# Joint steps of the second MLP product: the weight splits of a pair are ordered behind its first copy, and two slot splits move to a later place

## The chip, the cores and the metric

The kernel runs on one core of a Trainium2 chip. The metric is the device time of one execution in microseconds (us); the kernel before was timed three times, with a median of 2363.1 us (2361.05 to 2365.14).

The engines that matter here are TensorE (PE in the profile: matmuls, with their weight loads as PEld), VectorE (DVE), ScalarE (ACT), GpSimd (POOL, here only an issuer of DMAs) and SyncE (SP, which issues the weight loads).

## The reference

One decoder layer over 528 tokens of width 2048 (16 meta tokens and 512 real ones), in float32. Two token mixers are merged, and an MLP follows. The change touches only the second matrix product of that MLP.

```python
u2 = rmsnorm(h, norm2_g[l])
h = h + jnp.square(jax.nn.relu(u2 @ mlp_w1[l])) @ mlp_w2[l]
out = rmsnorm(h, final_g)
return out[:, N_META:]
```

`mlp_w1` is 2048 x 8192 and `mlp_w2` is 8192 x 2048. Calling the first product MLP 1 and the second MLP 2, MLP 2 is the stretch from about 1717 us to 2335 us of the profile.

## The kernel before, in words

**Three matmuls for one.** A float32 matmul is done with both operands split into a high part in a shorter format and a low remainder. `whi` and `wlo` are the parts of a weight block. A split costs one ScalarE copy (`whi <- raw`, line 154) and one VectorE subtraction (`wlo <- raw, whi`, line 155). The product is then high by high, high by low and low by high (`mm3`, line 396 in the profile).

**Seven products for eight.** The big products are done two by two blocks at a time with Winograd's form of Strassen's method. A group of four weight blocks a, b, c, d yields seven weight operands, in this order: a; s = c + d; s = s + a; b; c = c + a; s = s + b; d. The additions are on VectorE (line 142). Counting from 0, these are called split 0 to split 6. The seven products bear the name of the token-side operand: x11, t1, t2, x21, t3, x22, t4. They accumulate in the PSUM banks A, B, A, C, A, B, A. Results leave as follows: after x11 bank A is copied to `p1` (ScalarE); after t1 bank B is copied to `q5`; after t2 bank A is copied to `u2`; after x21 `put("11")` adds C and `p1`; after t3 `put("22")` combines A and `q5`; after x22 `put("12")` adds B and `u2`; after t4 `put("21")` is a negated copy on ScalarE.

**The weight stream.** The class `Weights` (lines 48 to 188) knows the loads and splits of the whole kernel in order. `next()` hands out the next pair of parts. `advance()` makes sure that the splits are traced up to two beyond the ones used. There are four buffers each for the loaded raw blocks, for `whi` and for `wlo`, and two for the sums. Each split that is traced also traces the loads that have a free buffer, on SyncE.

**MLP 2.** A step t takes a column of products along a diagonal. It uses the slots `max(0, t-8)` to `min(t, 31)-1`: step 1 has one slot, step 8 has eight. A slot holds the squared activations of two column blocks of MLP 1, in all the forms x11, t1 and so on. The slots come back from HBM by DMA (`load_slot`) and are split in place by `split_slot` (lines 1116 to 1121): one copy on ScalarE (line 1120) and one subtraction on VectorE (line 1121) for each of the pieces `x11` (256 columns), `late` (768: t1, x21, x22) and `soon` (768: t2, t4, t3).

**Joint steps.** Steps with few slots are done in pairs by `strassen_pair`, so that one split weight block serves both: first [1, 3] and [2, 4], and at the end [32, 38], [33, 37] and [34, 36]; between them come single steps 5 to 31 by `strassen`, and step 35 at last. In a pair the first step has `p1`, `u2`, `q5` in buffers of its own. The second step has them in the tile `scale`: its `p1` and its `q5` share one half of it, so that the copy of `q5` has to wait until `put("11")` has read `p1`. `scale` also holds the norm factor `rho` that MLP 1 reads until its last column. Below, "pair [1, 3]" and "pair [2, 4]" are the first two, and "step 3" the second step of the first of them.

**What precedes.** The last column of MLP 1 (j = 31, `strassen_turned`) starts MLP 2's work through the hooks in `last` (line 1127): it loads slots 1 to 3, splits slots 1 and 2, and after its last product traces four splits of weights ahead (`W.ready(W.used + 4)`). Its squared result `y` is stored by a DMA from a buffer that the results `e` of step 3 take over.

**The order on an engine.** The source isn't the order of execution. The framework arranges each engine's instructions when the program is built: of those that it deems ready it takes the one that comes first in the source, and one from further down goes ahead when nothing earlier is ready. In the trace, for instance, products of bank C of step 1 stand between two parts of a product in bank A. Each engine then executes its list in that order. `tc.issue_after(x)` adds an order: what the block traces on the engine of x is put behind x in that engine's list. It adds nothing on other engines.

**The places of the change.** `strassen_pair` (from line 795) calls `W.advance()` after each product. After the copy of `u2` it calls `between()`, which is `split_slot(n + 3)` (line 1202): slot 3 in pair [1, 3], slot 4 in pair [2, 4], and nothing in the last three pairs, where n + 3 is past the last slot. Slot 3 is first used by step 4 (second in pair [2, 4]), slot 4 by step 5. Results of the first two pairs are added to HBM in three pieces each by DMAs on POOL (line 1193), and a step's `e` buffer is free for a later step when these have landed.

Of the kernel before, what the change touches and what calls it, by code (L numbers as in the profile page):

```python
# [190 lines left out]
def build(ctx, tc, nc, xt_d, par_d, w_in_d, gate_d, pool_d, woa_d, wob_d, woc_d, w1_d, w2_d, w2t_d,  # L191
# [10 lines left out]
    W = Weights(nc, wpool, sums_pool, 4, 4)  # L202
# [82 lines left out]
    jobs = "V2_0 VL_2 VR_0 VL_3 GA_0 VP_2 GA_1 VP_3 VL_4 PW_0 VL_5 F_0 VP_4 GA_2 VP_5 F_1 VL_6 VP_6 VL_7 F_2"  # L285
    jobs += " VP_7 GA_3 VL_8 PW_1 F_3 VL_9 F_4 VP_8 GA_4 VP_9 VL_10 F_5 VP_10 VL_11 F_6 VP_11 GA_5 VL_12 PW_2 F_7"
    jobs += " VL_13 VP_12 GA_6 VP_13 VP_14 VL_14 VL_15 VP_15 GA_7 PW_3"
    jobs = [(j.split("_")[0], int(j.split("_")[1])) for j in jobs.split()]
# [35 lines left out]
    def slots_of(t):  # L324
        return range(max(0, t - WIN), min(t, JS))
# [67 lines left out]
    def mm3(o, w, mh, ml, first, last):  # L393
        wh, wl = w
        for i, (a, b) in enumerate(((wh, mh), (wh, ml), (wl, mh))):
            done = PE.matmul(o, a, b, start=first and i == 0, stop=last and i == 2, skip_group_check=True)  # L396
        return done
# [282 lines left out]
    def bank(name, j, n=HS):  # L680
        return ps.tile([P, 512], F32, tag="ps", name=f"ps_{name}{j}")[:, :n]
# [110 lines left out]
        put("21", E, u2)  # L792
        W.advance()

    def strassen_pair(names, jobs, puts, between):
        n = range(2)
        base = (0, len(jobs[0]("x11")))
        A, B, C = ([bank(x, name) for name in names] for x in "ABC")
        spare = {"p1": scale[:, :HS], "u2": scale[:, HS:SEQ], "q5": scale[:, :HS]}
        p1, u2, q5 = ([ep.tile([P, HS], F32, tag=x, name=f"{x}_{names[0]}"), spare[x]] for x in ("p1", "u2", "q5"))  # L800

        def product(os, r, first):
            hi, lo = W.next()
            for i in n:
                xs = jobs[i](r)
                for k, x in enumerate(xs):
                    s = slice((base[i] + k) * P, (base[i] + k + 1) * P)
                    mm3(os[i], (hi[:, s], lo[:, s]), *x, first and k == 0, k == len(xs) - 1)

        def put(c, os, zs):  # L810
            for i in n:
                puts[i](c, os[i], zs[i])

        def copy(os, xs):
            return [S.activation(o, x, AF.Copy) for o, x in zip(os, xs)][-1]

        product(A, "x11", True)
        copy(p1, A)
        W.advance()
        product(B, "t1", True)  # L820
        copy(q5[:1], B)
        W.advance()
        product(A, "t2", False)
        with tc.issue_after(copy(u2, A).ins):
            between()
        W.advance()
        product(C, "x21", True)
        put("11", C, p1)
        copy(q5[1:], B[1:])
        W.advance()  # L830
        product(A, "t3", False)
        put("22", A, q5)
        W.advance()
        product(B, "x22", False)
        put("12", B, u2)
        W.advance()
        product(A, "t4", False)
        put("21", A, (None, None))
        W.advance()

    def put_plain(e, by_half=False):

        def put(c, x, z):
            a, b = int(c[0]) - 1, int(c[1]) - 1
            n = 1 - a + 2 * b if by_half else 2 * a + b
            o = e[:, n * HS : (n + 1) * HS]
            if c[0] == "1":
                V.tensor_tensor(o, x, z, op=ALU.add)
            elif z is None:
                S.activation(o, x, AF.Copy, scale=-1.0)  # L850
            else:
                V.scalar_tensor_tensor(o, x, -1.0, z, op0=ALU.mult, op1=ALU.subtract)
        return put
# [238 lines left out]
    slots, early, n = {}, late.enter_context(ExitStack()), 14 * HS  # L1092
# [4 lines left out]
    def load_slot(j, queue):  # L1097
        if j < JS:
            s = slots[j] = places[j % (WIN + 1)]
            if j % (WIN + 1) in odd_places:  # L1100
                queue.dma_start(s[:, : 6 * HS].bitcast(F32), y_sp[j][:, : 6 * HS])
                queue.dma_start(s[:, 6 * HS + ODD : 7 * HS + ODD].bitcast(F32), y_sp[j][:, 6 * HS :])
            else:
                queue.dma_start(s[:, : 7 * HS].bitcast(F32), y_sp[j])

    def slot(j, r):

        s, odd = slots[j], j % (WIN + 1) in odd_places
        if r == "x11":
            lo = 6 * HS + (ODD if odd else 0)  # L1110
            return s[:, lo + HS : lo + 2 * HS], s[:, lo : lo + HS]
        a = {None: slice(0, 6 * HS), "late": slice(3 * HS, 6 * HS), "soon": slice(0, 3 * HS)}.get(r) or at(r)
        h = 8 * HS + (64 if odd else 0) + a.start
        return s[:, h : h + a.stop - a.start], s[:, a]

    def split_slot(j):
        if j < JS:
            for r in ("x11", "late", "soon") if j <= WIN else (None, "x11"):
                hi, lo = slot(j, r)
                S.activation(hi, lo.bitcast(F32), AF.Copy)  # L1120
                V.tensor_tensor(lo, lo.bitcast(F32), hi.bitcast(F32), op=ALU.subtract)
# [58 lines left out]
    def pair(q):  # L1180
        return ht[:, q].rearrange("p b a s -> p (b a s)")

    def of_slots(t):
        return lambda r: [slot(j, r) for j in slots_of(t)]

    def adding(e, p):
        put = put_plain(e, True)

        def put_and_add(c, x, z):
            put(c, x, z)  # L1190
            at = {"22": slice(HS, 3 * HS), "12": slice(3 * HS, 4 * HS), "21": slice(0, HS)}.get(c)
            if at:
                nc.gpsimd.dma_start(h_sp[p][:, at], e[:, at], accum_op=ALU.add)
        return put_and_add

    last = []
    for n, g in enumerate(groups):
        t = g[0]
        if len(g) > 1:
            es = [yp.tile([P, 2 * SEQ], F32, tag="ty"[i], name=f"e{x}") for i, x in enumerate(g)]  # L1200
            puts = [adding(e, x % WIN) if n < 2 else put_plain(e, True) for e, x in zip(es, g)]
            strassen_pair([f"b{x}" for x in g], [of_slots(x) for x in g], puts, lambda: split_slot(n + 3))
        else:
            es = [yp.tile([P, 2 * SEQ], F32, tag="yt"[t % 2], name=f"e{t}")]
            strassen(f"b{t}", of_slots(t), put_plain(es[0], True), between=lambda: split_slot(t) or [f() for f in last[::-1]])
        if n >= 2 and t < JS + 2:
            for x, e in zip(g, es):
                nc.gpsimd.dma_start(h_sp[x % WIN], e, accum_op=ALU.add)
        if n < 4:
            load_slot(n + 5, nc.gpsimd)  # L1210
        elif t >= WIN:
            load_slot(t + 1, nc.gpsimd)
        if t == JS + 2:
            ends.close()
            hp = ctx.enter_context(tc.tile_pool(name="hp2", bufs=1, reuse_waits="tile"))
            ht = hp.tile([P, KD // 2, 2, 2, HS], F32, name="acc")
            for q in (2, 0, 1, 3, 4, 5, 6, 7):
                nc.gpsimd.dma_start(pair(q), h_sp[ORDER[q]])
        if t >= JS + 2:
            for x, e in zip(g, es):  # L1220
                V.tensor_tensor(pair(x - JS), pair(x - JS), e, op=ALU.add)
        if t == JS + 2:
            fs, free = [], slots[25]
            for i, m in enumerate(range(2 * JS, 64)):
                yl, fh, fl = (free[:, (3 * i + x) * SEQ : (3 * i + x + 1) * SEQ] for x in range(3))
                nc.gpsimd.dma_start(yl.bitcast(F32), y_sp[m // 2][:, slice(0, SEQ) if m % 2 else slice(SEQ, 2 * SEQ)])
                fs.append((fh, fl))

                def split_last(yl=yl.bitcast(F32), fh=fh, fl=fl):
                    S.activation(fh, yl, AF.Copy)  # L1230
                    V.tensor_tensor(fl, yl, fh.bitcast(F32), op=ALU.subtract)
                last.append(split_last)
# [6 lines left out]
    n = 64 - 2 * JS  # L1239
# [121 lines left out]
```

## Time and profile before

| | |
|---|---|
| median of three runs | 2363.1 us |
| lowest and highest | 2361.05 and 2365.14 us |
| the profiled execution's own time | 2362.76 us |
| its span, first to last instruction | 2361.0 us |
| mean granted TensorE clock | 0.997 |
| PE busy, share of the span | 99% |
| DVE, ACT, POOL | 82%, 51%, 13% |

A row of the timeline gives start, duration, engine, line of the kernel, operation, output and inputs by the program's names with the numbers left out (`ps_Ab` is bank A of any step b1, b2 and so on), shapes, and how many were merged; in brackets the idle time of the engine before it and what ended that. The view of waits gives the total, the count and the longest. The view of windows gives the busy time of each engine in a stretch, with the number of instructions.

### The profile page before, as it was taken

The numbers are of one execution on the slowest core, as the hardware profiler recorded it, in microseconds if no ns is written. First come the engines' busy times: TensorE is split into PE (matmuls) and PEld (weight loads), VectorE is DVE, ScalarE is ACT, GpSimd is POOL, SyncE is SP. The second block draws the span as 40 slices with busy tenths as digits, with TensorE's granted clock in tenths as the row PEclk, the third lists the DMA queues.
The fourth block names the chain that finished last, engine by engine and source line by source line (L and its number), as shares of the span: only waits on it lengthen the run. The fifth ranks groups of instructions, "written<-read, shape, count | busy, mean of one in ns | idle before, by whom it ended". The sixth has DMA issues, their size and how long they took to land.

```text
span 2361.0 us, 46354 instructions
## 1 busy us (share of the span) xinstructions
PE 2334.7 (99%) x19274; PEld 2290.5 (97%) x19274; DVE 1927.0 (82%) x2375; ACT 1212.2 (51%) x1641; POOL 318.5 (13%) x439
## 2 busy tenths in 40 slices
PE   9999999999999999999999999999989999999997
PEld 9999999999999999888999999999989999999997
DVE  7866766698888886378989888888889888888877
ACT  6654545455555554244545444444455555555554
POOL 0224343300000000032000000000020000000013
PEclk9999999999999999999999999999999999999999
DMA  6255555754444447468545444555486666666663
GB/s 206 85 169 179 173 176 173 260 202 150 147 157 153 150 153 263 166 214 286 171 154 160 158 155 158 165 163 165 162 245 175 181 183 184 193 191 188 175 197 107
DMA packets 117442, 418.73 MB, mean 177 GB/s; under 512 B 14288, under 2 KB 19792, under 8 KB 115568
## 3 DMA queue, kind: packets, MB, share of 16 engines
q1 hardware_dynamic: 77472, 253.40, 33.5%
q0 software_dynamic: 39616, 162.29, 21.2%
q8 instruction: 150, 2.46, 0.4%
q14 instruction: 60, 0.49, 0.1%
q10 hardware_dynamic: 144, 0.10, 0.0%
HBM read 324.89 MB, written 90.31 MB: 176 GB/s over the span
## 4 chain that ended last, share of the span: by engine, by line
PE 86%; DVE 5%; issue 3%; DMA 2%; ACT 2%; POOL 2%; SPq 0%; POOLq 0%; ACTq 0%; DVEq 0%
PE ps_A L396 14%; PE ps_Ab L396 14%; PE ps_B L396 7%; PE ps_Bb L396 7%; PE ps_vp L396 5%; PE ps_vl L396 4%; PE ps_wo L396 4%; PE ps_Agp L396 4%; PE ps_Age L396 4%; PE ps_C L396 4%; PE ps_Agl L396 3%; PE ps_Cb L396 3%; PE ps_Bgp L396 2%; PE ps_Bgl L396 2%; PE ps_Bge L396 2%
## 5 line engine op out<-in xcount | busy, mean ns | idle before, releaser
L154 ACT ACTIVATE whi<-raw 128x1024 fp32r<-128x1024 f32 (+5 forms) x391 | 399.7, 1028 | 312.5 <-issue 80.4
L155 DVE TENSOR_TENSOR wlo<-raw,whi 128x1024 fp32r<-128x1024 f32 (+5 forms) x391 | 467.4, 1198 | 113.3 <-ACT whi L154 109.6
L154 ACT ACTIVATE whi<-sum 128x1024 fp32r<-128x1024 f32 (+3 forms) x267 | 279.0, 1045 | 449.3 <-DVE sum L142 231.0
L155 DVE TENSOR_TENSOR wlo<-sum,whi 128x1024 fp32r<-128x1024 f32 (+3 forms) x267 | 319.9, 1198 | 70.3 <-ACT whi L154 65.4
L396 PE MATMUL ps_A<-a,whi 128*128 128x256 f32 x2000 | 346.3, 277 | 0.6 <-ACT p L714 0.6
L396 PE MATMUL ps_Ab<-a,whi 128*128 128x256 f32 x1728 | 304.9, 277 | 0.0
L396 PEld LDWEIGHTS ps_A<-a,whi 128*128 128x128 f32 x2000 | 301.5, 188 | 1.4 <-ACT p L714 0.8
L396 PE MATMUL ps_A<-a,wlo 128*128 128x256 f32 x1000 | 276.5, 276 | 0.1
L396 PEld LDWEIGHTS ps_Ab<-a,whi 128*128 128x128 f32 x1728 | 260.9, 188 | 0.1
L396 PE MATMUL ps_Ab<-a,wlo 128*128 128x256 f32 x864 | 239.0, 277 | 0.0
L142 DVE TENSOR_TENSOR sum<-sum,raw 128x1024 f32<-128x1024 f32 (+4 forms) x178 | 213.7, 1201 | 5.7
L396 PEld LDWEIGHTS ps_A<-a,wlo 128*128 128x128 f32 x1000 | 187.7, 188 | 0.3 <-DVE wlo L155 0.3
L396 PE MATMUL ps_B<-a,whi 128*128 128x256 f32 x1024 | 177.7, 276 | 0.0
L396 PEld LDWEIGHTS ps_Ab<-a,wlo 128*128 128x128 f32 x864 | 162.5, 188 | 0.0
L396 PE MATMUL ps_vp<-a,whi 128*128 128x272 f32 (+1 forms) x896 | 160.4, 282 | 0.1
L396 PE MATMUL ps_vl<-a,whi 128*128 128x272 f32 (+1 forms) x896 | 160.2, 282 | 0.0
L396 PE MATMUL ps_wo<-a,whi 128*128 128x512 f32 x512 | 158.1, 390 | 0.0
L396 PEld LDWEIGHTS ps_B<-a,whi 128*128 128x128 f32 x1024 | 154.2, 188 | 0.2 <-ACT whi L154 0.2
L396 PE MATMUL ps_Bb<-a,whi 128*128 128x256 f32 x864 | 152.1, 276 | 0.0
L396 PE MATMUL ps_B<-a,wlo 128*128 128x256 f32 x512 | 141.5, 276 | 1.0 <-DVE wlo L155 1.0
L396 PEld LDWEIGHTS ps_vl<-a,whi 128*128 128x128 f32 x896 | 137.7, 188 | 0.2
L396 PEld LDWEIGHTS ps_vp<-a,whi 128*128 128x128 f32 x896 | 137.5, 188 | 0.3 <-ACT gs L540 0.3
(353 smaller groups left out, 5847.5 us busy)
## 6 DMA issues: line engine op xcount, KB each, us to landing
raw<-w SPq DMA_DIRECT2D x168, 512.0 KB, 4.2
raw<-w_in SPq DMA_DIRECT2D x134, 512.0 KB, 3.7
w<-w SPq DMA_DIRECT2D x56, 512.0 KB, 4.2
a<-ysp POOLq DMA_DIRECT2D x20, 896.0 KB, 6.2
ysp<-t POOLq DMA_DIRECT2D x31, 512.0 KB, 4.9
hsp<-e POOLq DMA_DIRECT2D x29, 512.0 KB, 5.8
w<-w_in SPq DMA_DIRECT2D x24, 512.0 KB, 4.0
ysp<-y POOLq DMA_DIRECT2D x31, 384.0 KB, 5.0
```

The source lines that it names most:

```text
L142: nc.vector.tensor_tensor(self.raw[o], self.raw[x], self.raw[y], op=ALU.add)
L154: nc.scalar.activation(hi[:, s], raw[:, s], AF.Copy)
L155: nc.vector.tensor_tensor(lo[:, s], raw[:, s], hi[:, s].bitcast(F32), op=ALU.subtract)
L396: done = PE.matmul(o, a, b, start=first and i == 0, stop=last and i == 2, skip_group_check=True)
```

## The change

`strassen_pair` gets one more argument, `when`. The `advance()` behind the first product is traced inside `issue_after` of the second step's `p1` copy. `between()` is still ordered behind the `u2` copy, but it is called at one of five places: 0 behind that copy as before, 1 behind result 11, 2 behind result 22, 3 behind result 12, 4 behind result 21. Pair [1, 3] takes 3, pair [2, 4] takes 4, and the last three pairs take 0.

```diff
-    def strassen_pair(names, jobs, puts, between):
+    def strassen_pair(names, jobs, puts, between, when):
...
+        def done(n, copied):
+            if n == when:
+                with tc.issue_after(copied.ins):
+                    between()
+
         product(A, "x11", True)
-        copy(p1, A)
-        W.advance()
+        with tc.issue_after(copy(p1, A).ins):
+            W.advance()
         product(B, "t1", True)
         copy(q5[:1], B)
         W.advance()
         product(A, "t2", False)
-        with tc.issue_after(copy(u2, A).ins):
-            between()
+        copied = copy(u2, A)
+        done(0, copied)
         W.advance()
         product(C, "x21", True)
         put("11", C, p1)
         copy(q5[1:], B[1:])
+        done(1, copied)
         W.advance()
         product(A, "t3", False)
         put("22", A, q5)
+        done(2, copied)
         W.advance()
         product(B, "x22", False)
         put("12", B, u2)
+        done(3, copied)
         W.advance()
         product(A, "t4", False)
         put("21", A, (None, None))
+        done(4, copied)
         W.advance()
...
-            strassen_pair(..., lambda: split_slot(n + 3))
+            strassen_pair(..., lambda: split_slot(n + 3), dict(enumerate((3,4))).get(n, 0))
```

More of the change, by code (lines that the diff above doesn't have):

```diff
@@ L1201, in build @@
             puts = [adding(e, x % WIN) if n < 2 else put_plain(e, True) for e, x in zip(es, g)]
-            strassen_pair([f"b{x}" for x in g], [of_slots(x) for x in g], puts, lambda: split_slot(n + 3))
+            strassen_pair([f"b{x}" for x in g], [of_slots(x) for x in g], puts, lambda: split_slot(n + 3), dict(enumerate((3,4))).get(n, 0))
         else:
```

## The prediction

> **What bounds the kernel now.** I read the page first, then the view of waits for TensorE, and then windows and timelines of the first joint steps.
>
> ```profile
> PE 2334.7 (99%) x19274; PEld 2290.5 (97%) x19274; DVE 1927.0 (82%) x2375; ACT 1212.2 (51%) x1641; POOL 318.5 (13%) x439
> ```
>
> ```profile
> PE ps_Bb L396 <- ACT scale L815: 2.4, 1, 2.4
> PE ps_Ab L396 <- ACT p_b L815: 2.3, 1, 2.3
> PE ps_Ab L396 <- DVE e L852: 1.6, 2, 1.2
> PE ps_Ab L396 <- ACT scale L815: 1.2, 1, 1.2
> ```
>
> TensorE is the bound, and nearly all that it loses in MLP 2 is lost in these four rows, 7.5 us together. The windows (columns: stretch, length, busy time with count per engine, granted clock, DMA share, GB/s) show where.
>
> ```profile
> core 0: us, PE busy (x) PEld busy (x) DVE busy (x) ACT busy (x) POOL busy (x), PEclk, DMA share, GB/s
> 1720.90:1743.70 22.80, 19.14 (x145) 18.33 (x145) 18.83 (x30) 16.45 (x32) 6.92 (x9) 0.93 0.95 268
> 1743.70:1750.90 7.20, 4.82 (x42) 4.63 (x42) 7.18 (x13) 1.37 (x4) 2.63 (x3) 1.00 0.51 131
> 1750.90:1762.10 11.20, 10.92 (x94) 10.71 (x93) 9.92 (x16) 8.39 (x15) 2.64 (x3) 1.00 0.99 229
> 1762.10:1794.00 31.90, 30.62 (x268) 30.43 (x268) 29.68 (x37) 18.33 (x28) 1.72 (x2) 1.00 0.59 162
> 1794.00:2344.00 550.00, 550.00 (x4834) 549.67 (x4835) 461.95 (x496) 292.20 (x406) 59.07 (x84) 1.00 0.60 176
> 1725.70:1729.40 3.70, 3.63 (x18) 3.64 (x19) 2.40 (x5) 3.10 (x8) 1.60 (x3) 0.55 0.92 297
> ```
>
> From 1794 on TensorE has no idle time for 550 us. What the change can win lies between 1720.9 and 1794, and there VectorE has little to spare: 7.18 of 7.20 us is busy in the second stretch and 29.68 of 31.90 in the fourth. In the last row 18 matmuls take 3.63 us at a granted clock of 0.55. At the rate of the long stretch (550.00 us over 4834, 0.114 us each) they would take 2.05, so the clock's fall behind the first two stalls costs 1.6 us more.
>
> **Part 1, the splits behind the first product's copy.** Pair [1, 3] has nothing in that block. The last hook of MLP 1 has already traced four splits ahead, and the `advance()` behind x11 asks for fewer. Its stalls look like this:
>
> ```profile
> 1722.28 0.63 ACT L154 ACTIVATE whi<-sum 128x512 fp32r<-128x512 f32 x1 [3.03 <-DVE sum L142]
> 1722.82 0.37 ACT L815 ACTIVATE p_b<-ps_Ab 128x256 f32<-128x256 f32 x1
> ...
> 1723.24 0.50 PE L396 MATMUL ps_Ab<-slot,whi 128*128 128x256 f32 x2 [2.32 <-ACT p_b L815]
> ...
> 1725.77 0.55 PE L396 MATMUL ps_Ab<-slot,whi 128*128 128x256 f32 x2 [1.19 <-ACT scale L815]
> ```
>
> The copy `p_b` stands behind a split that waits 3.03 us for a VectorE sum. That split was traced by the hook and not in the block, so it keeps its place, and 2.32 + 1.19 us of stall and the 1.6 us of slow clock stay. Moreover the product that waits, t2, uses this very split, which ends at 1722.28 + 0.63 = 1722.91. Cost and gain here: 0.
>
> In pair [2, 4] the block holds split 2, and that one already follows the copy:
>
> ```profile
> 1736.27 0.38 ACT L815 ACTIVATE scale<-ps_Ab 128x256 f32<-128x256 f32 x1
> 1736.53 0.85 ACT L154 ACTIVATE whi<-sum 128x768 fp32r<-128x768 f32 x1
> ```
>
> Again 0. In each of the last three pairs it does change the order. Here is pair [32, 38]:
>
> ```profile
> 2252.63 1.06 ACT L154 ACTIVATE whi<-sum 128x1024 fp32r<-128x1024 f32 x1 [2.64 <-DVE sum L142]
> ...
> 2253.73 1.23 DVE L155 TENSOR_TENSOR wlo<-sum,whi 128x1024 fp32r<-128x1024 f32 x1 [0.88 <-ACT whi L154]
> ...
> 2257.19 1.06 ACT L154 ACTIVATE whi<-w 128x1024 fp32r<-128x1024 f32 x1
> 2258.15 0.36 ACT L815 ACTIVATE scale<-ps_Ab 128x256 f32<-128x256 f32 x1
> ...
> 2259.77 0.39 PE L396 MATMUL ps_Ab<-a,whi 128*128 128x256 f32 x2
> 2259.99 0.28 PE L396 MATMUL ps_Ab<-a,wlo 128*128 128x256 f32 x1
> ```
>
> Split 2 is done at 2252.63, some 7 us before t2 needs it at 2259.77. The change puts it behind the copy into `scale`. That copy can start when x11 is done, about 2257.19 (there split 4 takes the buffer that x11 frees). Copy 0.36, `whi` 1.06 and `wlo` 1.23 end at 2259.84. The first third of t2's first block needs only `whi` (2258.61), and `wlo` is asked for at 2259.99: just in time. So the value that I take is 0, but the cover is gone. One VectorE instruction of 1.2 us in front makes it 1.1 late. If split 2 also finds its `whi` buffer taken by a later split, it waits until t1 is done (2259.77), and t2's `wlo` comes at 2259.77 + 1.06 + 1.23 = 2262.06, 2.1 late. TensorE can do x21 meanwhile, which has its own bank and weights; bounds are thus 0 and 2.1 per pair, 0 and 6.3 for three. A gain is excluded, as TensorE has no idle time there. I take 0, since the copy is short and the framework can turn products round.
>
> **Part 2, slot 3 behind result 12 of pair [1, 3].** No DMA moves with it, and POOL's adds and SP's loads keep their place in their own lists. On ScalarE it is still behind the `u2` copy, where nothing else is ready. On VectorE it now comes after results 11, 22 and 12:
>
> ```profile
> 1728.12 1.87 ACT L1120 ACTIVATE a<-a 128x256 fp32r<-128x256 f32 x3
> ...
> 1729.90 2.16 DVE L1121 TENSOR_TENSOR a<-a 128x256 fp32r<-128x256 f32 x3
> 1732.32 0.43 DVE L848 TENSOR_TENSOR e<-ps_Cb,scale 128x256 f32<-128x256 f32 x1 [0.26 <-DMA ysp<-y]
> ```
>
> The three subtractions (2.16 us) stand ahead of step 3's result 11, but that one waits 0.26 us longer for the store of MLP 1's last `y`, whose buffer it takes. So nothing is won on it: 0. Results of step 1 may go up to 2 us sooner, and with them the first adds to HBM; the slot's pieces come later by as much, for step 4's x11, which has other products in front. Bounds, as estimates: 1.0 won (sooner adds, half of those 2 us, since the later adds still follow their products) to 0.5 lost (one 0.42 us piece of the slot awaited); I take 0.
>
> **Slot 4 behind result 21 of pair [2, 4].** This is the step that matters.
>
> ```profile
> 1743.72 0.42 DVE L848 TENSOR_TENSOR e<-ps_Cb,p_b 128x256 f32<-128x256 f32 x1 [1.75 <-PE ps_Ab L396]
> 1744.06 0.42 DVE L1121 TENSOR_TENSOR a<-a 128x256 fp32r<-128x256 f32 x1
> 1744.39 0.95 DVE L155 TENSOR_TENSOR wlo<-raw,whi 128x768 fp32r<-128x768 f32 x1
> 1745.26 1.82 DVE L1121 TENSOR_TENSOR a<-a 128x768 fp32r<-128x768 f32 x2
> 1747.00 0.42 DVE L848 TENSOR_TENSOR e<-ps_Cb,scale 128x256 f32<-128x256 f32 x1
> ...
> 1747.45 0.39 ACT L815 ACTIVATE scale<-ps_Bb 128x256 f32<-128x256 f32 x1 [3.43 <-DVE e L848]
> ...
> 1747.89 0.50 PE L396 MATMUL ps_Bb<-slot,whi 128*128 128x256 f32 x2 [2.38 <-ACT scale L815]
> ```
>
> Step 4's result 11 (1747.00) frees `scale` for the `q5` copy, which frees bank B for x22: 0.89 us from the one to TensorE. Two subtractions of slot 4 (1745.26 to 1747.00) stand in front. Behind result 21 they come later, and result 11 starts at 1745.26: 1.74 us sooner, and the stall of 2.38 shrinks to 0.64. With the small piece gone too it is 0.33.
>
> But VectorE's work is only turned round. It is full until 1750.90, and the slot must be split before step 5 reaches its fifth slot. What is late next is step 5's weights:
>
> ```profile
> 1750.51 0.74 ACT L154 ACTIVATE whi<-sum 128x640 fp32r<-128x640 f32 x1
> 1751.28 0.83 DVE L155 TENSOR_TENSOR wlo<-sum,whi 128x640 fp32r<-128x640 f32 x1 [0.34 <-ACT whi L154]
> 1753.84 0.83 DVE L155 TENSOR_TENSOR wlo<-sum,whi 128x640 fp32r<-128x640 f32 x1 [0.87 <-ACT whi L154]
> ...
> 1762.13 0.50 PE L396 MATMUL ps_Ab<-slot,whi 128*128 128x256 f32 x2 [0.31 <-DVE e L852]
> ...
> 1793.97 0.50 PE L396 MATMUL ps_Ab<-slot,whi 128*128 128x256 f32 x2 [1.25 <-DVE e L852]
> ```
>
> At 1762.13 and 1793.97 TensorE waits for VectorE anyway. VectorE can be earlier there only by idle time that it loses: 11.20 - 9.92 = 1.28 us at most before 1762.1. The 0.34 is a wait for ScalarE, which stands behind a result of TensorE's that now comes sooner, so it goes; the 0.87 is a chain of sum, copy and subtraction and may stay. Kept: 0.34 to 1.28, and I take 0.8, the middle. The rest of the 1.74 comes back as waits for `wlo` in step 5 or for result 22 after it.
>
> Sum: 0 + 0 + 0 - 0.8. The profiled execution's 2362.76 becomes 2362.0; the median of the runs lies 0.3 above it, so 2362.3.
>
> On the clock, the Trainium skill ("TensorE: Matmul & The Clock Gate", Why this matters for your kernels) warns of "PE-idle gaps >~3µs between matmul bursts". By it neither the stalls here nor a late pair's 2.1 us would cost any clock; the trace disagrees, since gaps of 2.32 and 1.19 us sufficed for the 0.55.
>
> **The rivals.**
> *The whole stall is kept.* If step 1's earlier adds let VectorE start sooner than 1743.72 (it idles 1.75 us there), or the framework's new list also turns results ahead of splits in steps 5 and 7, the three late waits may go: 2.38 alone is 2360.7, and 2.38 + 0.31 + 1.25 = 3.9 is 2359.2. For it: that idle time. Against it: VectorE's full windows.
> *The order hardly changes.* The framework takes a ready split when nothing earlier is ready, and did so at 1744.06 to 1745.26. Then the two pieces stay in front of result 11: 2363.1.
> *Slower: split 2 is late in the last three pairs.* It decides when `wlo` of split 2 ends after 2259.99, that is, with more than 0.15 us of anything between the copy and it. At 1.1 per pair, 3.3 - 0.8 gives 2365.6; at 2.1, 6.3 - 0.8 gives 2368.6, and each stall may bring a fall of the clock as above. For it: a later split takes a freed buffer first at 2257.19, ahead of the copy. Against: x21 can fill in.
> The Trainium skill speaks against the change here ("TensorE: Matmul & The Clock Gate", Architectural detail): ScalarE and VectorE are strictly first in, first out, so whatever is behind a waiting copy waits as well. Row 1747.45 agrees, with 3.43 us in which ScalarE did nothing.
>
> **How the numbers follow.** A measurement of this kernel can tell about 0.2%, 4.7 us, from no change. Forecast 0.52 (its own range, with the spread of the runs, 2360.8 to 2364.2), whole stall kept 0.17, order as before 0.13, slower 0.18. The range is from 2359.5, inside the second case, to 2367.0, inside the last. Faster than 2358.4 needs more than all three late waits, or the spread of the runs on top of them: 0.06. Slower than 2367.8 needs the dear half of the last case: 0.09. The rest, 0.85, is within.
>
> **What would show it.** Right: the waits of 2.3 and 1.2 us and the slow-clock stretch at 1726 unchanged; `e<-ps_Cb,scale` of step 4 near 1745 and the wait of `ps_Bb` for `scale` at 0.7 us or less; after 1794 the same matmuls about 0.8 us sooner. In the last pairs `whi<-sum` directly behind the second copy, with no idle time on TensorE. Wrong: `p_b` of step 1 sooner than 1722.8, or any TensorE wait for `wlo` or `whi` after 2250.

## The result and the profile after

The change makes the kernel slower: 2367.54 us (2366.35 to 2373.82, 8 runs) against 2363.01 us (2360.49 to 2365.14, 8 runs), a ratio of 1.0025 with a 95% interval of 1.0016 to 1.0034. That is 4.5 us more, and 0.5 us above the top of the predicted range.

The profiled execution after the change took 2373.82 us, the longest of its eight and 6.3 above their median. So it isn't compared end to end but stretch by stretch. It was 5.85 us late before the change begins: the first product of pair [1, 3] starts at 1723.65 instead of 1717.80, and up to there every engine has the same list of instructions in both kernels. A part of this is the second row here, 3.0 us where the profile of before has 0.5. Slow clock makes up about the rest: TensorE ran at half the clock for 6.8 us at 276 instead of 3.4, and for 3.4 us at 1119, where before has none. The view of waits for TensorE, after (total, count, longest):

```profile
PE ps_Ab L396 <- DVE wlo L155: 3.8, 1, 3.8
PE ga L396 <- ACT xs L525: 3.0, 1, 3.0
PE ps_Ab L396 <- ACT p_b L815: 2.1, 1, 2.1
PE ps_Ab L396 <- DVE e L861: 1.7, 1, 1.7
...
PE ps_Ab L396 <- ACT scale L815: 1.1, 1, 1.1
...
PE ps_Ab L396 <- ACT whi L154: 0.6, 1, 0.6
...
PE ps_Bb L396 <- DVE wlo L155: 0.2, 1, 0.2
```

Beside the four rows of before: `ps_Bb <- scale` (2.4) is gone; `p_b` and `scale` stay, as forecast; the two waits for `e` (0.31 and 1.25 before) are one of 1.7; 0.6 and 0.2 us for weights of step 5 are new; and at the top stands one wait for `wlo` that before doesn't have at all.

Two stretches divide the matter. The first goes from the start of pair [1, 3] to the last resumption of TensorE in step 7, which the prediction quoted at 1793.97: 76.17 us before, 75.72 after. The second goes from there to the first matmul of the last norm: 540.72 before, 546.41 after. So the first joint steps got 0.45 us shorter, and the late ones 5.7 us longer. The 0.45 is too small a figure for the change: behind the first stalls the clock was at half for 6.8 us after and for 3.4 before, which alone is 1.7 us, so with the same clock the first steps would, as an estimate, be 2.2 us shorter. In the late stretch, TensorE after:

```profile
2284.29 0.39 PE L396 MATMUL ps_Ab<-a,whi 128*128 128x256 f32 x2
2288.43 0.39 PE L396 MATMUL ps_Ab<-a,wlo 128*128 128x256 f32 x1 [3.75 <-DVE wlo L155]
```

This is t2 of pair [33, 37]: two matmuls that need only `whi` are done, and the third waits 3.75 us for the `wlo` of split 2. Behind it the clock falls (window: length, PE busy with count, PEld, DVE, ACT, POOL, granted clock, DMA share, GB/s):

```profile
2288.40:2293.00 4.60, 4.57 (x26) 4.57 (x26) 3.38 (x3) 0.77 (x3) 2.88 (x6) 0.63 1.00 341
```

At the prediction's 0.114 us each, 26 matmuls are 2.96 us; they took 4.57, so the clock costs another 1.6. Together 5.35 of the 5.7.

Why `wlo` comes late is seen by setting ScalarE and VectorE side by side. ScalarE after:

```profile
2281.77 0.39 ACT L815 ACTIVATE scale<-ps_Ab 128x256 f32<-128x256 f32 x1 [0.32 <-PE ps_Ab L396]
2282.05 1.06 ACT L154 ACTIVATE whi<-sum 128x1024 fp32r<-128x1024 f32 x1
```

VectorE after:

```profile
2284.76 1.23 DVE L142 TENSOR_TENSOR sum<-w,raw 128x1024 f32<-128x1024 f32 x1 [7.00 <-DMA raw<-w]
2286.02 1.22 DVE L142 TENSOR_TENSOR w<-w,raw 128x1024 f32<-128x1024 f32 x1
2287.16 1.22 DVE L155 TENSOR_TENSOR wlo<-sum,whi 128x1024 fp32r<-128x1024 f32 x1
```

`whi` of split 2 follows the copy directly, as intended, and is done at 2283.11. With VectorE free, `wlo` would end at 2283.11 + 1.22 = 2284.33, before TensorE asks for it at 2284.68. VectorE is indeed idle, for 7.00 us, but its next instruction is another: the first addition of the *next* group of four blocks, which waits for the load of a raw block. Two additions and then `wlo` follow. In the kernel before, the same addition waits for the same load, but split 2 is already done. VectorE before:

```profile
2272.81 1.23 DVE L155 TENSOR_TENSOR wlo<-sum,whi 128x1024 fp32r<-128x1024 f32 x1 [0.54 <-ACT whi L154]
...
2278.75 1.23 DVE L142 TENSOR_TENSOR sum<-w,raw 128x1024 f32<-128x1024 f32 x1 [2.32 <-DMA raw<-w]
```

The added order binds only ScalarE. As the lists read, the low part of split 2 became ready later for the framework, behind the copy, and the additions went ahead of it on VectorE.

The list is turned in the same way in the other late pairs. In pair [32, 38] VectorE waits for a load too, after:

```profile
2261.50 1.22 DVE L142 TENSOR_TENSOR sum<-w,raw 128x1024 f32<-128x1024 f32 x1 [3.24 <-DMA raw<-w]
2262.76 1.23 DVE L142 TENSOR_TENSOR w<-w,raw 128x1024 f32<-128x1024 f32 x1
2264.02 1.22 DVE L155 TENSOR_TENSOR wlo<-sum,whi 128x1024 fp32r<-128x1024 f32 x1
```

There `wlo` ends at 2265.24, and the matmul that needs it starts at 2265.40: it cost nothing by 0.16 us.

### The profile page after: what moved, and what is told of

Same layout as the page of the kernel before. It is cut to its first block, busy times and chain, and to the rows that moved or that the text cites. A ratio compares the mean times of both kernels' runs of the same rounds, so it can differ in the third digit from the quotient of the medians.

```text
span 2372.1 us, 46340 instructions
## 1 busy us (share of the span) xinstructions
PE 2341.4 (99%) x19274; PEld 2296.8 (97%) x19274; DVE 1925.4 (81%) x2375; ACT 1211.3 (51%) x1641; POOL 318.2 (13%) x439
## 4 chain that ended last, share of the span: by engine, by line
PE 58%; issue 21%; DVE 3%; DMA 3%; POOL 2%; ACT 1%; POOLq 0%; SPq 0%; DVEq 0%; ACTq 0%
PE ps_Ab L396 13%; PE ps_Bb L396 6%; PE ps_wo L396 4%; PE ps_Age L396 4%; PE ps_Agp L396 4%; PE ps_vp L396 3%; PE ps_Agl L396 3%; PE ps_Cb L396 3%; PE ps_vl L396 3%; PE ps_A L396 2%; PE ps_Bge L396 2%; PE ps_Bgp L396 2%; PE ps_Bgl L396 2%; DMA raw<-w 1%; PE ga L396 1%
## 5 line engine op out<-in xcount | busy, mean ns | idle before, releaser
L142 DVE TENSOR_TENSOR sum<-w,raw 128x1024 f32<-128x1024 f32 (+3 forms) x89 | 106.4, 1196 | 40.9 <-DMA raw<-w 40.0
```

Of the source, the lines that this page charges most:

```text
L142: nc.vector.tensor_tensor(self.raw[o], self.raw[x], self.raw[y], op=ALU.add)
```

## The experiments

Theory "late": the loss is this stall and its clock, caused by VectorE's list. Rival "early": the loss comes from the moved slot splits or from the first pairs. The first four kernels took one part of the change each, or mended the suspected list.

**1. Part 2 alone** (both slot splits moved, no added order):

```diff
-        with tc.issue_after(copy(p1, A).ins):
-            W.advance()
+        copy(p1, A)
+        W.advance()
```

> Only the two slot splits move; the block behind the first product's copy has no added order. Theory late (the loss comes from the last three pairs, where the low part of split 2 stands on VectorE behind additions that wait for a load): the stall of 3.75 us near 2288 and the fall of the clock after it are gone, the early pairs are 0.5 to 2 us quicker, so 2361 to 2362.6 where the kernel before has 2363. Rival early (the loss comes from the moved slot splits, by a longer slow-clock stretch and a fuller VectorE in the first pairs): about 2367, as with the whole change.

**2. Part 1 alone** (added order in all pairs, slots split where they were):

```diff
-... lambda: split_slot(n + 3), dict(enumerate((3,4))).get(n, 0))
+... lambda: split_slot(n + 3), 0)
```

> Only the order behind the first product's copy; the slot splits stay where they were. Theory late: the waits of the first pairs are as before, and the pair [33, 37] stalls for 3 to 4 us on the low part of split 2, with 1.7 us of slow clock behind it: 2366.5 to 2368.5. Rival early: within 1 us of before, 2363.

**3. The order in the first two pairs only**, with part 2:

```diff
-        with tc.issue_after(copy(p1, A).ins):
+        copied1 = copy(p1, A)
+        with tc.issue_after(copied1.ins) if names[0] in ("b1", "b2") else contextlib.nullcontext():
             W.advance()
```

> The whole change, but the added order in the pairs [1, 3] and [2, 4] alone. Theory late: no stall after 2250, 2361 to 2362.6, like the moved slot splits alone to within 1 us. Rival early: about 2367.

**4. The whole change, with the next group's additions ordered behind split 2's low part on VectorE** in the last three pairs (`lows[i]` keeps the subtraction of split i; `behind` is a hook that the kernel has around additions):

```diff
...
+        late = W.used + 1
         with tc.issue_after(copy(p1, A).ins):
             W.advance()
+        if len(jobs[0]("x11")) > 4:
+            W.behind = lambda i: tc.issue_after(W.lows[late].ins) if i in (late + 6, late + 9) else contextlib.nullcontext()
```

> The whole change, and in the last three pairs the next group's two additions (sum and w) are ordered on VectorE behind the low part of split 2. Theory late, with the additions as its cause: the low part no longer waits for the load that the sum waits for, the stall of 3.75 us falls below 0.5, and the time is 2361 to 2363. If the copy's lateness itself were the cause (the high part done only after the t2 product could start): a stall of 1 us or more in each of the three pairs stays, 2366 or more.

Measured, each against the kernel before on the same chip (2361.26 us). The expectations were written with 2363 us for the kernel before, so it is the differences that count. The two stretches are those of above, from one profiled execution each. In the first stretch the clock was at half for 3.4 us in the profiles of before and of kernels 2, 4, 5, 6, 10 and 12, and for 6.8 us in those of after and of kernels 1, 3, 7, 8, 9 and 11; that alone is 1.7 us between them.

| kernel | us | ratio, 95% interval | first stretch | late stretch |
|---|---|---|---|---|
| before (its own profile) | | | 76.17 | 540.72 |
| after (its own profile) | | | 75.72 | 546.41 |
| 1 part 2 alone | 2359.35 | 0.9993 [0.9984, 1.0002] | 73.24 | 540.87 |
| 2 part 1 alone | 2367.22 | 1.0026 [1.0016, 1.0037] | 75.41 | 546.95 |
| 3 order in first pairs | 2359.97 | 0.9995 [0.9986, 1.0004] | 75.35 | 540.82 |
| 4 additions behind | 2360.09 | 0.9998 [0.9989, 1.0007] | 74.71 | 540.91 |

Part 1 alone has the whole loss, and a wait of 2.9 us for `wlo` in pair [33, 37]. Its lists show how far the order reaches: by names and shapes they are those of before on every engine up to 2250 us; in each of the last three pairs those of ScalarE and VectorE differ; and not one of TensorE's 19274 matmuls has another place. Kernel 4 keeps every order of the change and adds only the one on VectorE, and VectorE's is the only list that differs from the changed kernel's; its late stretch is that of before again. Its VectorE in pair [33, 37]:

```profile
2274.76 1.23 DVE L155 TENSOR_TENSOR wlo<-sum,whi 128x1024 fp32r<-128x1024 f32 x1 [4.42 <-ACT whi L154]
...
2278.18 1.22 DVE L142 TENSOR_TENSOR sum<-sum,raw 128x1024 f32<-128x1024 f32 x1
2279.31 1.22 DVE L142 TENSOR_TENSOR sum<-w,raw 128x1024 f32<-128x1024 f32 x1
```

Now VectorE waits for ScalarE's `whi` and for nothing else, and the addition that waited for a load comes after it without any idle time. "Early" falls: kernels 1 and 3 hold all that it could blame, and lost nothing.

Next: is it one pair or all three, what sets the length of the wait, and was the claim on pair [1, 3] right?

**5. The order in pair [33, 37] only**, and **6. in [32, 38] and [34, 36] only**, both with part 2; the edit is that of kernel 3 with other names.

> The two slot splits in their new places, the added order in pair [33, 37] alone. Theory 'one pair': the whole loss of the added order lies here, since only in this pair has VectorE's list the next group's sum, which waits for a DMA, ahead of split 2's low part. It expects a wait of ps_Ab for wlo of 2.9 to 3.8 us in this pair, 1.7 us of slow clock behind it, and with the 2359.35 of the kernel without added order 2364 to 2365.5. Rival 'three pairs': each of the three pairs loses something that the waits of the other two don't show. It expects less than half of the loss, under 2362.

> The two slot splits in their new places, the added order in pairs [32, 38] and [34, 36] alone. Theory 'one pair' expects no wait of TensorE between 1800 and the last norm, and the time of the kernel without added order, 2359.4 within 1.5. Rival 'three pairs' expects 2362 or more.

**7. Two splits ahead instead of four in MLP 1's last hook**, otherwise kernel 3:

```diff
-            "t4": lambda: (split_slot(2), W.ready(W.used + 4))}
+            "t4": lambda: (split_slot(2), W.ready(W.used + 2))}
```

> The whole change with the added order only in the first two pairs, and the last hook of MLP 1 traces two splits ahead instead of four, so that in pair [1, 3] too split 2 is in the block behind the copy. The prediction's claim was that a sooner p_b gains nothing, since t2 needs that very split: then the wait of 2.2 us for p_b becomes one of 1.9 to 2.3 us for whi or wlo at the same place, and the time is 2360.0 (the kernel with four ahead) within 1.5. Rival: with p_b sooner TensorE does x21 and t1 of step 3 first, the wait shrinks to under 0.8 us and the slow clock behind it goes: 2357.5 or less. Third: fewer splits ahead make step 1's later weights late, new waits for wlo, over 2362.

**8. The whole change, the loads of `acc` later** on GpSimd's queue:

```diff
-                nc.gpsimd.dma_start(h_sp[x % WIN], e, accum_op=ALU.add)
+                added = nc.gpsimd.dma_start(h_sp[x % WIN], e, accum_op=ALU.add)
...
-                nc.gpsimd.dma_start(pair(q), h_sp[ORDER[q]])
+                with tc.issue_after(added.ins):
+                    nc.gpsimd.dma_start(pair(q), h_sp[ORDER[q]])
```

> The whole change, but the loads of acc on GpSimd are ordered behind the two additions of pair [32, 38] to HBM, so that fewer bytes are under way while the raw block of the next group is loaded. Theory 'late': the stall ends when that load lands. In the changed kernel it landed 7.2 us after its issue at 2277.52; the two acc loads issued at 2276.87 and 2277.42 would go out some 3 us later. If it is their traffic that delays it, it lands 4 to 6 us after its issue, the stall of 3.75 us shrinks to 0.5 to 2.5, and the time is 2363 to 2366. Rival: the load is slow for another reason (its own queue, or the additions to HBM), the stall stays over 2.9 us, and the time stays at 2367.

| kernel (before: 2361.68 us) | us | ratio, 95% interval | first stretch | late stretch |
|---|---|---|---|---|
| 5 order in [33, 37] | 2365.43 | 1.0015 [1.0007, 1.0024] | 74.06 | 545.73 |
| 6 order in [32, 38], [34, 36] | 2363.18 | 1.0005 [0.9996, 1.0014] | 73.58 | 542.80 |
| 7 two splits ahead | 2366.65 | 1.0019 [1.0010, 1.0028] | 79.12 | 540.73 |
| 8 `acc` loads later | 2364.14 | 1.0011 [1.0002, 1.0019] | 75.52 | 544.01 |

*Kernel 5* has the stall (3.10 us) and the slow clock, and is at the top of what "one pair" expected. *Kernel 6* contradicts "one pair": it has a stall too, in pair [34, 36], of 1.12 us. TensorE and VectorE there:

```profile
2297.49 0.38 PE L396 MATMUL ps_Ab<-a,wlo 128*128 128x256 f32 x1 [1.12 <-DVE wlo L155]
```

```profile
2294.88 0.69 DVE L142 TENSOR_TENSOR sum<-w,raw 128x512 f32<-128x512 f32 x1 [1.60 <-DMA raw<-w]
2295.60 0.69 DVE L142 TENSOR_TENSOR w<-w,raw 128x512 f32<-128x512 f32 x1
2296.21 1.22 DVE L155 TENSOR_TENSOR wlo<-sum,whi 128x1024 fp32r<-128x1024 f32 x1
```

The same two additions stand in front of `wlo`. In the changed kernel TensorE doesn't wait here, and the additions of [34, 36] start at 2305.76 with no idle time ahead of them: the longer wait in [33, 37] gave the load time to land. So the place is "each pair where the next group's load isn't there in time", and the stalls of two pairs don't add up. Its late stretch is 2.1 us longer than that of before; 1.12 are the wait, and the rest lies in a slower pace of matmuls (last section).

*Kernel 8* shows what sets the length. The raw block in front of [33, 37]: in the changed kernel its load was issued at 2277.15 in two parts, among loads of `acc` (SyncE and GpSimd, after):

```profile
2277.15 1.69 SPq L125 DMA_DIRECT2D raw<-w  x2
2276.87 1.10 POOL L1227 DMA_DIRECT2D acc<-hsp  x2 [15.44 <-PE ps_Ab L396]
```

and VectorE could use it at 2284.76, 7.6 us later. In kernel 8, SyncE and VectorE:

```profile
2268.97 1.42 SPq L125 DMA_DIRECT2D raw<-w  x2
```

```profile
2272.76 1.23 DVE L142 TENSOR_TENSOR sum<-w,raw 128x1024 f32<-128x1024 f32 x1 [3.19 <-DMA raw<-w]
2274.02 1.23 DVE L142 TENSOR_TENSOR w<-w,raw 128x1024 f32<-128x1024 f32 x1
2275.17 1.22 DVE L155 TENSOR_TENSOR wlo<-sum,whi 128x1024 fp32r<-128x1024 f32 x1
```

In both kernels the load was issued 3.92 us ahead of the copy `p_b`, and GpSimd's is the only list that differs. With `acc` out of the way the load takes 3.8 us, and the stall in [33, 37] is gone, where 0.5 to 2.5 us of it had been expected to stay. As in kernel 6 a stall then shows in [34, 36], of 1.34 us, and the kernel stays 2.5 us over the one before.

*Kernel 7* came out as its third case, and shows a part of the prediction's claim on pair [1, 3]. Its waits for TensorE:

```profile
PE ps_Ab L396 <- ACT whi L154: 3.3, 3, 2.1
PE ps_Ab L396 <- DVE wlo L155: 1.9, 1, 1.9
```

The wait for `p_b` is gone, as that copy now runs at 1718.47, and one of 2.05 us for `whi` stands in its place, up to 1724.61: t2 needs that split, whatever the copy does. That the size is the one expected is luck. The sum for this `whi` is done at 1721.28, but ScalarE's list has the squaring of MLP 1's last `y` ahead of it, which waits 3.86 us for VectorE and starts at 1722.72. x21 of step 1 does go ahead of t2, as the rival said, without its gain. The later splits are late as well, and the first stretch grows to 79.12.

The last four part the small gain of the slot splits, and try for more.

**9. Slot 3 moved alone** (`(3,0)` in the call, no added order), **10. slot 4 alone** (`(0,4)`), **11. both, once more** (kernel 1), and **12. both, with the order in the last hook turned round**:

```diff
-            "t4": lambda: (split_slot(2), W.ready(W.used + 4))}
+            "t4": lambda: (W.ready(W.used + 4), split_slot(2))}
```

> Slot 3 behind result 12 alone; slot 4 and the weight splits as before. The prediction's 0 for this step: the waits for p_b, for scale in step 3 and the 2.4 us of ps_Bb for scale in pair [2, 4] stay, and the time is that of the kernel before within 1. Rival: with slot 3 later the adds of step 1 go out sooner and VectorE is less late throughout, 1 us or more won, and the wait of ps_Bb for scale shrinks here already.

> Slot 4 behind result 21 alone; slot 3 and the weight splits as before. The prediction's step: the wait of ps_Bb for scale falls from 2.4 us to 0.7 or less, 0.8 us of it is kept, 0.3 to 1.3 being the bounds. Rival 'kept whole': 1.7 us or more below before, with no new wait in step 5 or 7. Rival 'order unchanged': the wait of 2.4 us stays.

> Both slot splits moved, no added order, once more and beside each part alone. If the two moves add up and nothing else plays in, its difference to before is the sum of the other two, 0.8 to 2.5 us won (1.9 was measured the first time).

> Both slot splits moved, no added order, and the last hook of MLP 1 traces its four weight splits ahead of slot 2's split instead of behind it. In the kernel with both slots moved VectorE did 1.4 us of slot 2 between the landing of the raw block at 1718.46 and the sum that split 2 and, behind it, the copy p_b wait for. Theory: this order is what holds the 1.6 to 2.3 us of the first stall. It expects p_b within 0.5 us of the end of x11, the first stall under 0.8 us, and 0.5 to 3 us less than without this swap, the more if the slow clock behind the stall goes too. Rival: slot 2's parts, now later, stall step 3's t1 by as much: the same time.

| kernel (before: 2362.67 us) | us | ratio, 95% interval | first stretch | late stretch |
|---|---|---|---|---|
| 9 slot 3 alone | 2361.20 | 0.9995 [0.9984, 1.0005] | 74.26 | 541.77 |
| 10 slot 4 alone | 2363.29 | 1.0003 [0.9994, 1.0012] | 75.75 | 540.82 |
| 11 both | 2360.54 | 0.9991 [0.9982, 1.0000] | 73.41 | 541.66 |
| 12 both, hook turned | 2361.29 | 0.9993 [0.9984, 1.0002] | 75.84 | 540.72 |

No interval tells these from each other, so what follows for kernels 9 and 10 is read from traces. Nor can the sum be tested that kernel 11 was to show: the two moves alone come to 0.85 us won, both together to 2.13. In kernel 9 the 2.38 us of `ps_Bb` waiting for `scale` in pair [2, 4] is 0.28 already, by slot 3's move alone, which was the rival's sign. VectorE there:

```profile
1739.14 0.42 DVE L857 TENSOR_TENSOR e<-ps_Cb,p_b 128x256 f32<-128x256 f32 x1
...
1742.72 0.42 DVE L857 TENSOR_TENSOR e<-ps_Cb,scale 128x256 f32<-128x256 f32 x1
```

Step 4's result 11 still comes 3.58 us behind step 2's, since slot 4 is still between them (before: 1743.72 and 1747.00, 3.28). But step 2's result no longer finds VectorE idle for 1.75 us ahead of it, as before: the framework also gave TensorE another list there. In kernel 10 the two results follow each other by 1.20 us, just as the prediction worked it out, and the wait for `scale` is 0.3 at that place. But step 5 gives it back:

```profile
PE ps_Ab L396 <- ACT whi L154: 0.6, 1, 0.6
PE ps_Bb L396 <- DVE wlo L155: 0.6, 2, 0.4
...
PE ps_Ab L396 <- DVE wlo L155: 0.4, 1, 0.4
```

Kernel 12's rival won: the same time. The wait for `p_b` is gone, and two others came, for slot 2's parts (already at step 3's x11, not at its t1) and for a longer hold of `scale`:

```profile
PE ps_Bb L396 <- ACT scale L815: 2.2, 1, 2.2
PE ps_Ab L396 <- DVE e L861: 1.9, 3, 1.1
PE ps_Ab L396 <- DVE a L1130: 1.7, 1, 1.7
PE ps_Ab L396 <- ACT scale L815: 1.5, 1, 1.5
```

The best version is part 2 alone: 1.9 and 2.1 us under the kernel before in two sets of runs, each interval just reaching 1. That isn't enough to call it faster.

## Why the prediction was wrong, point by point

**The step that failed** is the last one of part 1: "I take 0, since the copy is short and the framework can turn products round", with 0 and 2.1 us per pair as bounds. Its arithmetic was right as far as it went. `whi` stands directly behind the copy, and with VectorE free `wlo` ends 0.35 us before it is needed; kernel 4 made that so and the loss was gone. What failed is the silent assumption that VectorE *is* free for `wlo`. The text named the danger ("One VectorE instruction of 1.2 us in front makes it 1.1 late") but never looked at what stands next in VectorE's list in each of the three pairs. It argued from [32, 38] alone, and its rows leave out the same two additions there, which in before run at 2257.27 and 2258.52 without a wait. Nor did the framework turn products round: TensorE's list stayed as it was. Row 2278.75 of before, in [33, 37], was there to be read: an addition with 2.32 us idle ahead of it, ended by a DMA. An instruction that waits for a load and costs nothing where it stands becomes the price as soon as something needed is put behind it. The real price was 3.75 us, above the bound, once and not three times, plus 1.6 us of clock, which the prediction named ("each stall may bring a fall of the clock as above") and didn't add. A wait of TensorE for `wlo` after 2250 was its own sign of being wrong, and it came. A smaller slip: 2252.63 is the start of split 2's copy and not its end; `wlo` ended at 2254.96, so the cover in before was 5 us and not 7.

**The rival "slower"** had the mechanism, the right condition (anything over 0.15 us between the copy and `wlo`) and, at 2368.6, a time near the measured 2367.5. That nearness is luck, as it adds three stalls of 2.1 us without the clock where one of 3.75 with the clock came. It had the wrong cause for its dear end (a `whi` buffer) and too small a chance. "Against: x21 can fill in" did not hold: the list of TensorE has t2 ahead of x21, and TensorE waited.

**Part 1 in the first two pairs.** Void in [1, 3]: right, and kernel 7 shows that t2 does wait for that split with `p_b` long copied. In before `p_b` ended at 1723.19 and `whi` at 1722.91, so 0.3 us was the most to be won. "Again 0" in [2, 4] was right for part 1 alone, where the lists there are those of before. It was wrong for the whole change: with the slots moved, split 2 stands ahead of the copy, and the order turns them. ScalarE in kernel 1, then in kernel 3:

```profile
1734.66 0.85 ACT L154 ACTIVATE whi<-sum 128x768 fp32r<-128x768 f32 x1
1735.41 0.37 ACT L815 ACTIVATE scale<-ps_Ab 128x256 f32<-128x256 f32 x1
```

```profile
1734.80 0.39 ACT L815 ACTIVATE scale<-ps_Ab 128x256 f32<-128x256 f32 x1 [0.54 <-PE ps_Ab L396]
1735.08 0.84 ACT L154 ACTIVATE whi<-sum 128x768 fp32r<-128x768 f32 x1
```

VectorE then waits 1.03 us for this `whi`, and step 5 for its weights, three times, 1.2 us in all. In the four profiles with both slots moved, the hook as before and no order there, the first stretch was 73.24 and 73.41 us (6.8 us of slow clock) and 73.58 and 74.06 (3.4); in the four that have the order, 75.35, 75.52 and 75.72 (6.8) and 74.71 (3.4). But the medians of kernels 3 and 4 lie only 0.6 and 0.7 us above kernel 1's, on one chip, less than the runs can tell, so what the order costs there is not settled.

**Part 2.** Predicted 0.8 won; measured 1.9 and 2.1 with intervals that hold both 0 and 0.8. The stall of 2.38 us vanished instead of shrinking to 0.64. The split into terms was probably wrong: slot 3, taken at 0, seems to bring more than slot 4, whose gain goes to step 5 as described ("comes back as waits for `wlo` in step 5").

**What stayed.** The waits for `p_b` and `scale` in pair [1, 3], 2.1 and 1.1 us after against 2.3 and 1.2, though with 6.8 us of slow clock behind them and not 3.4; and no gain after 1794 that part 2 could have made.

## What to carry to other kernels

An order that is added on one engine can change the lists of others: before moving an instruction, read what stands next in the list of every engine of its chain, in each place where the edit applies, and look for instructions that wait there for a DMA at no cost today. A cover that is 0.15 us thin should be priced by what stands in front of it at worst, with the fall of the clock added, and not by the duration of the chain alone.

## What the runs showed of the hardware

*A load's time depended on its neighbours.* The same two-part load of a raw block was usable 7.6 us after its issue among loads of `acc`, and 3.8 us without them, in one profile each.

*Clock.* Waits of 2.91, 3.10 and 3.75 us in [33, 37] each brought about 3.4 us at half the clock; waits of 1.12 and 1.34 us in [34, 36] brought none, nor did the single one of 2.38 us in pair [2, 4] of before. Two waits close together needed less: 1.56 and 0.82 us in pair [1, 3] of kernel 1 brought 6.8 us of it. At the first two stalls of pair [1, 3] the slow stretch was 3.4 us in some executions and 6.8 in others, with waits alike (2.32 and 1.19 us before: 3.4; 2.06 and 1.12 after: 6.8). At half the clock the difference is 1.7 us. The Trainium skill ("TensorE: Matmul & The Clock Gate", HAM oscillation — how this bites in real kernels) sets the limit at idle gaps of about 3.4 us; the gaps of 2.91 and 3.10 us here were enough, so the measurement decides.

*Pace at full clock.* In kernel 6 two neighbouring windows, with no idle time of TensorE and the granted clock at 1.00 in both, hold different counts:

```profile
2240.00:2257.00 17.00, 17.00 (x152) 17.00 (x151) 10.08 (x11) 6.41 (x10) 0.86 (x1) 1.00 0.54 132
2257.00:2274.00 17.00, 17.00 (x147) 17.00 (x146) 14.98 (x19) 9.49 (x15) 2.84 (x5) 1.00 0.50 158
```

That is 0.112 and 0.116 us per matmul, 3% apart. Products of 24 matmuls took 2.72 us in one and 2.83 in the other. The same slower pace stands behind the stall of kernel 8, from 2300 to 2335. What causes it stays open; it is enough to add 1 to 2 us to a single profile. Kernels 9 and 11 have late stretches 1 us longer than before's with no wait at all.
